# A two-layer hybrid decoder on one core: the first stage's input array in groups of eight partitions

## The chip, the cores and the metric

One of the eight cores of a Trainium2 chip runs the whole kernel. The metric is the time of one execution on the device in microseconds (us), and less is better. On the core, TensorE multiplies matrices, VectorE and ScalarE do element-wise work, GpSimd a little of it, and 16 DMA engines move data between the chip's memory (HBM) and the on-chip memory (SBUF, 128 partitions). SyncE (SP) only issues transfers; ScalarE has a queue for them too.

## The reference

Two layers of the same form, then a final normalisation, on x of 256 tokens by 1024 features, all in float32:

```python
hn = rms_norm(x, norm_gain)
proj = jnp.einsum('bsd,de->bse', hn, w_in)          # 1024 -> 3584
a_q, a_k, a_v, a_g, b_x, b_g, c_q, c_k, c_v, c_g = jnp.split(proj, _in_split_points(), axis=-1)
...
y_a = dilated_attention(qa, ka, va)... * jax.nn.silu(a_g)
y_b = rg_lru_branch(b_x, ...) * jax.nn.silu(b_g)
y_c = stick_breaking_attention(qc, kc, vc)... * jax.nn.silu(c_g)
y = jnp.concatenate([y_a, y_b, y_c], axis=-1)
return x + jnp.einsum('bse,ed->bsd', y, w_out)
```

The first stage of the kernel is two column blocks of the first layer's projection: a_v (512 columns) and c_v (256 columns), the values of the two attentions.

## The kernel before

Float32 products are made from two rounded parts each: a high part, rounded by ScalarE, and the rest, subtracted by VectorE; TensorE then adds three products (high by high, rest by high, high by rest). The kernel works through weight chunks, each loaded by SP in two halves of 512 KB into one of five staging buffers `st`, split into `whi` and `wlo`, and multiplied. TensorE's order is the order of the code; the other engines' is settled by the scheduler. A load waits until its staging buffer has been read.

The first stage runs over the 1024 features in eight tiles of 128 (`NK`, loop variable `k`), one feature a partition. A tile holds, per partition, 256 numbers of x transposed and 768 weights, 4 KB. Tile 0 comes in small pieces so that work can begin early: x with the eight columns of the norm's gain (`x0`, 264 numbers a partition, line 138), then three blocks of 256 weights (lines 139 to 141, two of them on ScalarE's queue). Tiles 1 to 7 come whole, each 512 KB, issued by SP at line 152. For each tile ScalarE rounds x times the gain into `xx` (line 161) and the weights or part of them into `whi` (lines 165 and 167), VectorE takes the rests (lines 163, 168, 170), and TensorE multiplies at line 181. Ahead of the stage TensorE runs seven multiplications of zeros (line 147).

Two arrays in HBM feed this stage: `first_x`, 128 rows of 264 numbers, and `first`, eight tiles of 128 rows of 1024 numbers, each row the 256 numbers of x and the 768 weights of one feature. Line 138 reads the first whole; lines 139 to 141 read 256 numbers of each of the 128 rows of tile 0; line 152 reads a whole tile, 128 rows that follow each other:

```python
nc.sync.dma_start(out=x0, in_=first_x)
act.dma_start(out=st0[:, S:S + 256], in_=first[0][:, S:S + 256])
...
        nc.sync.dma_start(out=st, in_=first[k])
```

After the stage SP goes on with the small parameters (line 186), the first weight chunks (line 108), the residual x (line 191), constants and rotation tables (lines 196 and 422). In each layer GpSimd issues two copies of half the partitions from one buffer on the chip to another (line 593).

Of the kernel before, what the change touches and what calls it, by code (L numbers as in the profile page):

```python
# [15 lines left out]
P = 128  # L16
S = 256
# [3 lines left out]
NK = D // P  # L21
# [11 lines left out]
STORE = (0, 256, 640, 1024)  # L33
WARM = 7

C_DG = 0
C_ID = 127
C_NM = 256
# [8 lines left out]


@with_exitstack
def trunk_kernel(ctx: ExitStack, tc: tile.TileContext, x, first_x, first, wpack, prm_d, gatew, gains, consts, rope, out):  # L50
    nc = tc.nc
    act, dve, pe, gps = nc.scalar, nc.vector, nc.tensor, nc.gpsimd

# [23 lines left out]
    def table(name, behind=()):  # L77
        load = act.preload_act_table_set(name)  # L78
        for u in (*loaded["users"], *behind):
            dep(load, u)  # L80
        loaded["load"], loaded["users"] = load, []
# [48 lines left out]
    def weights(l, c, ahead=AHEAD):  # L130
        ask(l, c, ahead)
        return ready.pop((l, c))
# [2 lines left out]
    dve.memset(cold, 0.0)  # L135
    x0 = sb.tile([P, S + NK], F32, name="x0", tag="it")
    st0 = wst.tile([P, 1024], F32, name="st", tag="st")
    nc.sync.dma_start(out=x0, in_=first_x)
    act.dma_start(out=st0[:, S:S + 256], in_=first[0][:, S:S + 256])
    nc.sync.dma_start(out=st0[:, S + 256:S + 512], in_=first[0][:, S + 256:S + 512])  # L140
    act.dma_start(out=st0[:, S + 512:1024], in_=first[0][:, S + 512:1024])
    table(LN_EXP)
    av_ps = [bank(at, "s") for _ in range(NT)]
    cv_bk = [bank(pp, "pp") for _ in range(NT)]
# [4 lines left out]
    for k in range(NK):  # L149
        st = st0 if k == 0 else wst.tile([P, 1024], F32, name="st", tag="st")  # L150
        if k > 0:
            nc.sync.dma_start(out=st, in_=first[k])
        x_in = x0 if k == 0 else st
        g = x0[:, S + k:S + k + 1]
        if k % 2 == 0:
            pair = [wsp.tile([P, 2048], F32R, name=n, tag=n) for n in ("whi", "wlo")]
        o = k % 2
        hi, cl, lo = pair[0][:, o * 1024:o * 1024 + 768], pair[0][:, o * 1024 + 768:o * 1024 + 1024], pair[1][:, o * 512:o * 512 + 512]
        both = pair[0][:, o * 1024 + 512:o * 1024 + 1024]
        w = st[:, S:1024]  # L160
        act.activation(xh[:, k, :], x_in[:, 0:S], AF.Copy, scale=g)  # L161
        for c0, c1 in {0: ((0, 256), (256, 512)), 1: ((0, 512),)}.get(k, ()):
            dve.tensor_copy(hi[:, c0:c1], w[:, c0:c1])
        if k < 2:
            act.activation(hi[:, 512:768], w[:, 512:768], AF.Copy)
        else:
            act.activation(hi, w, AF.Copy)
        dve.scalar_tensor_tensor(xl[:, k, :], x_in[:, 0:S], g, xh[:, k, :].bitcast(F32), ALU.mult, ALU.subtract)
        for rest, c0, c1 in ((lo, 0, 512), (cl, 512, 768)):
            dve.tensor_sub(rest, w[:, c0:c1], hi[:, c0:c1].bitcast(F32))  # L170
        cuts = (0, 256, 512) if k == 0 else (0, 512)
        av = [[(av_ps, c0, c1, a, b[:, c0:c1]) for c0, c1 in zip(cuts, cuts[1:])]
              for a, b in ((xh, hi), (xl, hi), (xh, lo))]
        cv = [[(cv_bk, 0, 256, a, hi[:, 512:768])] for a in (xh, xl)] + [[(cv_bk, 256, 512, xh, cl)]]
        if k < 2:
            seq = [m for i in range(3) for m in (*av[i], *cv[i])]
        else:
            seq = [m for i in range(3) for m in av[i]] + [(cv_bk, 0, 512, xh, both), *cv[1]]
        for i, (ps, c0, c1, a, b) in enumerate(seq):
            for t in range(NT):  # L180
                pe.matmul(ps[t][:, c0:c1], a[:, k, t * P:(t + 1) * P], b,  # L181
                          start=k == 0 and all(m[0] is not ps for m in seq[:i]),
                          stop=k == NK - 1 and all(m[0] is not ps for m in seq[i + 1:]), skip_group_check=True)
# [10 lines left out]
    nmask = con[:, C_NM:C_NM + 384]  # L194
    diag = con[:, C_DG:C_DG + 255]
    nc.sync.dma_start(out=con, in_=consts)
# [114 lines left out]
    for l in range(L):  # L311
# [394 lines left out]
        for n2 in range(2):  # L706
            w = weights(l, CH_O + n2)
# [41 lines left out]
def _shape_constants():  # L749
    f = np.float32  # L750
    con = np.zeros((P, C_W), f)
    con[:, C_ID:C_ID + P] = np.eye(P, dtype=f)
    nm = np.full((P, 384), -8 * BIG, f)
    for t0, c0, n in ((0, 0, 128), (128, 128, 256)):
        d = (t0 + np.arange(P))[:, None] - np.arange(n)[None, :]
        c = (d <= 128).astype(int) + (d % 4 == 0) + (d % 16 == 0)
        c = np.where(d >= 0, c, 0)
        nm[:, c0:c0 + n] = np.where(c > 0, 8 * np.log(np.maximum(c, 1).astype(np.float64)), -8 * BIG)
    con[:, C_NM:C_NM + 384] = nm
    return con  # L760
# [17 lines left out]
def _pack_weights(w_in, w_out):  # L778
    wp = np.empty((L, NCH, P, 2048), np.float32)
    narrow = ((CH_CV, 3072), (CH_BX, 2048), (CH_BG, 2304), (CH_AG, 1536), (CH_AG + 1, 1792), (CH_CG, 3328),  # L780
              (CH_CQ, 2560), (CH_CK, 2816), (CH_AQ[0], 0), (CH_AQ[1], 256), (CH_AK[0], 512), (CH_AK[1], 768))
    yk = (6, 7, 4, 5, 0, 1, 2, 3)
    for l in range(L):
        wi = w_in[l].reshape(NK, P, 3584)
        for h in range(2):
            wp[l, CH_AV + h] = wi[4 * h:4 * h + 4, :, 1024:1536].transpose(1, 0, 2).reshape(P, 2048)
        for c, col in narrow:
            blk = wi[:, :, col:col + 256]
            if c in CH_AQ + CH_AK:
                blk = blk.reshape(NK, P, 4, 2, 32).transpose(0, 1, 3, 2, 4).reshape(NK, P, 256)  # L790
            wp[l, c] = blk.transpose(1, 0, 2).reshape(P, 2048)
        wo = w_out[l].reshape(NK, P, D)
        for h in range(2):
            for n in range(2):
                blk = np.stack([wo[k, :, n * 512:n * 512 + 512] for k in yk[4 * h:4 * h + 4]])
                wp[l, CH_O + 2 * h + n] = blk.transpose(1, 0, 2).reshape(P, 2048)
    return wp


def _pack_small(conv_w, conv_b, gate_a_w, gate_a_b, gate_x_w, gate_x_b, lru_lambda):  # L800
    pr = np.zeros((P, L * SM_P), np.float32)
    gw = np.zeros((P, L, SM_W), np.float32)
    for l in range(L):
        for b in range(2):
            r = slice(b * P, b * P + P)
            o = l * SM_P + 8 * b
            pr[:, o:o + 4] = conv_w[l][:, r].T
            pr[:, o + 4] = conv_b[l][r]
            pr[:, o + 5] = gate_a_b[l].reshape(-1)[r]
            pr[:, o + 6] = gate_x_b[l].reshape(-1)[r]  # L810
            pr[:, o + 7] = lru_lambda[l][r]
            for g, w in enumerate((gate_a_w, gate_x_w)):
                c = (g * 2 + b) * P
                for j in range(2):
                    gw[(j ^ g) * HD:((j ^ g) + 1) * HD, l, c + j * HD:c + (j + 1) * HD] = w[l, 2 * b + j]
    return pr, gw


def _arrays(x, norm_gain, w_in, conv_w, conv_b, gate_a_w, gate_a_b, gate_x_w, gate_x_b,
            lru_lambda, w_out, final_gain):  # L820
    x, norm_gain, w_in, conv_w, conv_b, gate_a_w, gate_a_b, gate_x_w, gate_x_b, lru_lambda, w_out, final_gain = [
        np.asarray(a) for a in (x, norm_gain, w_in, conv_w, conv_b, gate_a_w, gate_a_b, gate_x_w, gate_x_b,
                                lru_lambda, w_out, final_gain)]
    x2 = x.reshape(S, D)
    pr, gw = _pack_small(conv_w, conv_b, gate_a_w, gate_a_b, gate_x_w, gate_x_b, lru_lambda)
    return {
        "x_in": np.ascontiguousarray(x2),
        "first_x": np.concatenate([x2.T[0:P], norm_gain[0].reshape(NK, P).T], 1),
        "first": np.concatenate([x2.T.reshape(NK, P, S), w_in[0].reshape(NK, P, 3584)[:, :, 1024:1536],
                                 w_in[0].reshape(NK, P, 3584)[:, :, 3072:3328]], 2),  # L830
        "w_pack": _pack_weights(w_in, w_out),
        "prm": pr,
        "gate_w": gw,
        "gains": np.concatenate([norm_gain[1:], final_gain[None]], 0),
        "consts": _shape_constants(),
        "rope": _rope_table(),
    }
# [16 lines left out]
```

## Time and profile before

| what | value |
|---|---|
| median of three runs | 246.11 us (246.09 to 246.35) |
| the profiled execution's own time | 246.06 us |
| its span, first to last instruction | 244.2 us |
| TensorE busy | 236.2 us (97%) |
| VectorE, ScalarE busy | 200.0 us (82%), 174.4 us (71%) |
| moved by DMA | 43.89 MB, mean 180 GB/s |
| granted TensorE clock | 0.999 |

In the rows below PE is TensorE's matmul, PEld its weight load, DVE VectorE, ACT ScalarE, POOL GpSimd, SP SyncE; a `q` behind an engine's name is its queue of transfers. L152 is line 152. A row of the timeline has start, length, engine, line, operation and tiles (written <- read), and in brackets the engine's idle time before it with what ended that.

### The profile page before, as it was taken

The page shows a single profiled execution, that of the slowest core. Times are in us where ns is not written, and L with a number is a line of the kernel's source. Part 1 is how long each engine was busy: PE and PEld are TensorE (multiplying, and loading weights), DVE is VectorE, ACT ScalarE, POOL GpSimd, SP SyncE. Part 2 cuts the span into 40 slices and gives each one's busy share as a digit, 9 for nine tenths or more (in the row PEclk, how much of TensorE's full clock was granted, in tenths as well). Part 3 has the DMA queues.
Part 4 walks back from the last instruction along what each step waited for, and adds up shares of the span by engine and source line. Part 5 has one row for each costly group of instructions (what it writes and reads, how often), then busy time and mean ns, then how long its engine had stood idle before and what let it go on. Part 6 is the DMA issues. An engine that isn't in the chain of part 4 may idle for free.

```text
span 244.2 us, 4576 instructions
## 1 busy us (share of the span) xinstructions
PE 236.2 (97%) x1651; PEld 206.6 (85%) x1651; DVE 200.0 (82%) x480; ACT 174.4 (71%) x384; POOL 10.5 (4%) x43
## 2 busy tenths in 40 slices
PE   8799999999999999999999999999999999999991
PEld 4588999999999798878888888888888878887881
DVE  3694699999999889999495585999999986997362
ACT  3677987919597689994673674876669867998143
POOL 0017200002000000000000000000010000000000
PEclk9999999999999999999999999999999999999999
DMA  6989988565846843068448288615470771000022
GB/s 193 377 254 390 384 268 291 190 205 177 240 152 207 272 153 105 1 195 320 175 134 273 88 289 268 199 44 177 171 214 7 226 282 63 31 0 0 3 75 97
DMA packets 14037, 43.89 MB, mean 180 GB/s; under 512 B 1728, under 2 KB 3008, under 8 KB 14016
## 3 DMA queue, kind: packets, MB, share of 16 engines
q1 hardware_dynamic: 13248, 42.43, 51.9%
q0 software_dynamic: 192, 0.52, 0.8%
q10 hardware_dynamic: 576, 0.66, 0.7%
q8 instruction: 13, 0.21, 0.4%
q14 instruction: 8, 0.07, 0.1%
HBM read 42.03 MB, written 1.05 MB: 176 GB/s over the span
## 4 chain that ended last, share of the span: by engine, by line
PE 94%; DMA 3%; DVE 1%; SPq 0%; ACT 0%; issue 0%; DVEq 0%
PE pp L225 34%; PE pp L344 20%; PE pp L341 10%; PE s L225 9%; PE s L181 4%; PE s L489 3%; DMA st<-first 3%; PE y L453 2%; PE pp L383 2%; PE s L542 2%; PE pp L181 2%; PE s L469 1%; PE y L225 1%; PE pp L453 1%; PE s L601 1%; PE s L273 1%
## 5 line engine op out<-in xcount | busy, mean ns | idle before, releaser
L117 DVE TENSOR_TENSOR wlo<-st,whi 128x512 fp32r<-128x512 f32 x128 | 81.8, 684 | 7.5 <-ACT whi L115 6.9
L115 ACT ACTIVATE whi<-st 128x512 fp32r<-128x512 f32 x130 | 72.5, 627 | 9.0 <-DMA st<-w_pack 3.4
L344 PE MATMUL pp<-xx,whi 128*128 128x512 f32 x208 | 50.8, 393 | 0.0
L344 PEld LDWEIGHTS pp<-xx,whi 128*128 128x128 f32 x208 | 37.8, 188 | 7.6 <-DVE q L349 0.3
L225 PE MATMUL pp<-xx,whi 128*128 128x256 f32 x288 | 38.2, 285 | 0.0
L225 PEld LDWEIGHTS pp<-xx,whi 128*128 128x128 f32 x288 | 35.8, 191 | 0.8 <-issue 0.3
L341 PEld LDWEIGHTS pp<-xx,wlo 128*128 128x128 f32 x208 | 26.9, 191 | 1.6 <-ACT scr L84 0.3
L341 PE MATMUL pp<-xx,wlo 128*128 128x256 f32 x208 | 28.0, 284 | 0.0
L225 PE MATMUL pp<-xx,wlo 128*128 128x256 f32 x144 | 20.2, 283 | 0.0
L84 ACT ACTIVATE pr<-scr,mn 128x128 f32<-128x128 f32 (+1 forms) x32 | 14.1, 443 | 6.6 <-DVE mn L549 6.6
L225 PEld LDWEIGHTS pp<-xx,wlo 128*128 128x128 f32 x144 | 18.6, 192 | 0.0
L78 ACT ACT_TABLE_LOAD x13 | 16.7, 1283 | 1.9 <-PEq L847 1.7
L347 ACT ACTIVATE low<-pp 128x256 f32<-128x256 f32 x26 | 9.4, 373 | 8.8 <-PE pp L344 8.0
L225 PE MATMUL pp<-whi,yh 128*128 128x512 f32 (+1 forms) x48 | 14.1, 382 | 0.0
L225 PE MATMUL pp<-wlo,yh 128*128 128x512 f32 (+1 forms) x48 | 13.7, 372 | 0.0
L225 PE MATMUL pp<-whi,yl 128*128 128x512 f32 (+1 forms) x48 | 13.6, 371 | 0.0
L181 PE MATMUL s<-whi,xx 128*128 128x512 f32 (+1 forms) x36 | 9.6, 384 | 1.8 <-ACT xx L161 1.7
L225 PEld LDWEIGHTS pp<-whi,yl 128*128 128x128 f32 x48 | 8.6, 188 | 1.6
L225 PEld LDWEIGHTS pp<-wlo,yh 128*128 128x128 f32 x48 | 8.6, 188 | 1.6
L225 PEld LDWEIGHTS pp<-whi,yh 128*128 128x128 f32 x48 | 8.3, 188 | 1.6 <-issue 0.3
L549 DVE CUSTOM_DVE_ANT_0 scr<-s,con 128x128 f32<-128x128 f32 (+1 forms) x32 | 9.2, 350 | 0.0
L181 PEld LDWEIGHTS s<-whi,xx 128*128 128x128 f32 x36 | 6.0, 197 | 3.3 <-ACT xx L161 2.5
(189 smaller groups left out, 372.3 us busy)
## 6 DMA issues: line engine op xcount, KB each, us to landing
st<-w_pack SPq DMA_DIRECT2D x66, 512.0 KB, 5.3
st<-first SPq DMA_DIRECT2D x7, 512.0 KB, 7.0
xres<-x_in SPq DMA_DIRECT2D x4, 256.0 KB, 7.5
gw_t<-gate_w SPq DMA_DIRECT2D x2, 256.0 KB, 6.8
gn<-gains SPq DMA_DIRECT2D x2, 256.0 KB, 5.9
xs<-xc POOLq DMA_DIRECT2D x4, 128.0 KB, 3.8
gf<-gains SPq DMA_DIRECT2D x2, 256.0 KB, 5.4
out<-st ACTq DMA_DIRECT2D x2, 192.0 KB, 2.0
```

The lines of the kernel that those rows point to most:

```text
L78: load = act.preload_act_table_set(name)
L84: i = dep(act.activation(*a, **k), loaded["load"])
L115: split[l, c] = act.activation(h, part, AF.Copy)
L117: dve.tensor_sub(r, part, h.bitcast(F32))
L181: pe.matmul(ps[t][:, c0:c1], a[:, k, t * P:(t + 1) * P], b, start=k == 0 and all(m[0] is not ps for m in seq[:i]), stop=k == NK - 1 and al ...
L225: pe.matmul(ps, a(k), b(k), start=first and i == 0, stop=last and i == len(seq) - 1, skip_group_check=skip)
L341: pe.matmul(ps[:, 0:S], lo[:, k, cs], xh[:, k, :], start=i == 0, stop=i == len(seq) - 1, skip_group_check=True)
L344: pe.matmul(ps, hi[:, k, cs], xx[:, k].rearrange("p h t -> p (h t)"), start=i == 0, stop=i == len(seq) - 1, skip_group_check=True)
L347: act.activation(low, ps[:, S:2 * S], AF.Copy, scale=sc)
L453: pe.matmul(y[hr, p * 128 + o:p * 128 + 256], vt[:, s0, hs], wts[i][s0], start=s0 == 0, stop=s0 == 1)
L489: pe.transpose(tp[:, i * P:(i + 1) * P], tiles[h0 + h][:, j * P:(j + 1) * P], ident)
L549: dve.tensor_tensor_reduce(xs[:, cs], sps[h][:, cs], nmask[:, cs], -0.125, 3e38, ALU.add, ALU.min, mn[:, t:t + 1])
```

## The change

The two arrays become one, `first`, of 16 rows of 66,624 numbers (266,496 bytes). Row e holds everything that partitions 8e to 8e + 7 get in the first stage, in the order in which it is loaded: their eight rows of x with the gain, their eight rows of the first block of 256 weights, of the second and of the third, and then for each of the seven tiles their eight rows of 1024. At its end stand 1024 zeros. Each load takes a stretch of all 16 rows and reads it as 16 x 8 rows into 128 partitions. What is loaded into which place, in which order and on which queue stays as it was.

```diff
+FIRST_W = 8 * (NK + NK * 1024) + 1024
...
-    nc.sync.dma_start(out=x0, in_=first_x)
-    act.dma_start(out=st0[:, S:S + 256], in_=first[0][:, S:S + 256])
-    nc.sync.dma_start(out=st0[:, S + 256:S + 512], in_=first[0][:, S + 256:S + 512])
-    act.dma_start(out=st0[:, S + 512:1024], in_=first[0][:, S + 512:1024])
+    def block(q, to, at_, n):
+        q.dma_start(out=to, in_=first[:, 8 * at_:8 * (at_ + n)].rearrange("e (r c) -> e r c", r=8))
+
+    block(nc.sync, x0, 0, S + NK)
+    block(act, st0[:, S:S + 256], S + NK, 256)
+    block(nc.sync, st0[:, S + 256:S + 512], S + NK + 256, 256)
+    block(act, st0[:, S + 512:1024], S + NK + 512, 256)
...
-            nc.sync.dma_start(out=st, in_=first[k])
+            block(nc.sync, st, NK + k * 1024, 1024)
...
+def _pack_first(xt, gain, wi):
+    w = np.concatenate([wi[:, :, 1024:1536], wi[:, :, 3072:3328]], 2)
+    parts = [np.concatenate([xt[0], gain.reshape(NK, P).T], 1), w[0, :, 0:256], w[0, :, 256:512], w[0, :, 512:768]]
+    parts += [np.concatenate([xt[k], w[k]], 1) for k in range(1, NK)]
+    rows = [a.reshape(P // 8, -1) for a in parts]
+    flat = np.concatenate(rows, 1)
+    out = np.zeros((P // 8, FIRST_W), np.float32)
+    out[:, 0:flat.shape[1]] = flat
+    return out
```

The arrays are laid out ahead of the launch. In the order of instructions, SP's queue at the start of the program stands so before (a row is a line, the transfer's target and source, and the target's shape as the instruction carries it):

```order
L138 DMA x_84<-first_x 128x264
L140 DMA st<-first 128x256
L152 DMA st<-first 128x1024 x7
L186 DMA prm_t<-prm 128x32
L108 DMA st<-w_pack 128x1024 x2
```

and so with the change:

```order
L140 DMA x_84<-first 128x1x264
L140 DMA st<-first 128x1x256
L140 DMA st<-first 128x1x1024 x7
L190 DMA prm_t<-prm 128x32
L109 DMA st<-w_pack 128x1024 x2
```

No transfer has moved; the shapes of the first stage's transfers have a level more, and the lines behind have shifted by a few. ScalarE's two transfers change in the same way, and the other engines' orders are the same.

More of the change, by code (lines that the diff above doesn't have):

```diff
@@ L49, in trunk_kernel @@
 @with_exitstack
-def trunk_kernel(ctx: ExitStack, tc: tile.TileContext, x, first_x, first, wpack, prm_d, gatew, gains, consts, rope, out):
+def trunk_kernel(ctx: ExitStack, tc: tile.TileContext, x, first, wpack, prm_d, gatew, gains, consts, rope, out):
     nc = tc.nc
@@ L827, in _arrays @@
         "x_in": np.ascontiguousarray(x2),
-        "first_x": np.concatenate([x2.T[0:P], norm_gain[0].reshape(NK, P).T], 1),
-        "first": np.concatenate([x2.T.reshape(NK, P, S), w_in[0].reshape(NK, P, 3584)[:, :, 1024:1536],
-                                 w_in[0].reshape(NK, P, 3584)[:, :, 3072:3328]], 2),
+        "first": _pack_first(x2.T.reshape(NK, P, S), norm_gain[0], w_in[0].reshape(NK, P, 3584)),
         "w_pack": _pack_weights(w_in, w_out),
```

## The prediction

> **What bounds the kernel now.** I read the busy times first, then the stages, then the one wait that the stages point to, then the transfers behind that wait. Of the stage rows the first number is the length, the second TensorE's busy time; the last two are the busy share of the DMA engines and the rate in GB/s.
>
> ```profile
> span 244.2 us, 4576 instructions
> PE 236.2 (97%) x1651; PEld 206.6 (85%) x1651; DVE 200.0 (82%) x480; ACT 174.4 (71%) x384; POOL 10.5 (4%) x43
> ...
> 4.10:6.80 2.70, 2.69 (x19) 2.46 (x18) 1.63 (x4) 0.42 (x1) 0.00 (x0) 1.00 0.85 302
> 6.80:8.50 1.70, 0.02 (x1) 0.04 (x1) 0.56 (x2) 0.59 (x2) 0.00 (x0) 1.00 1.01 410
> 8.50:23.40 14.90, 14.82 (x72) 12.33 (x73) 12.35 (x29) 11.58 (x23) 4.79 (x14) 1.00 0.94 326
> 23.40:60.00 36.60, 36.60 (x336) 35.70 (x335) 32.84 (x71) 28.07 (x57) 2.80 (x16) 1.00 0.73 258
> 60.00:120.00 60.00, 60.00 (x448) 53.02 (x445) 53.84 (x140) 46.69 (x108) 1.21 (x3) 1.00 0.58 189
> 120.00:236.00 116.00, 116.00 (x754) 99.23 (x753) 94.22 (x223) 82.21 (x185) 1.31 (x3) 1.00 0.40 130
> ```
>
> TensorE is the bound at full clock: from 8.5 to 236 us it never stands still. The one hole inside the work is 6.8 to 8.5. Whatever moves the end of that hole moves the end of the kernel by as much, in both directions; an earlier end is worth 1.69 us at most. The timeline says what ends it:
>
> ```profile
> 3.51 0.51 ACT L161 ACTIVATE xx<-x 128x256 fp32r<-128x256 f32 x1 [0.56 <-DMA x<-first_x]
> 4.13 0.92 PE L181 MATMUL s<-whi,xx 128*128 128x256 f32 x4
> ...
> 7.91 0.51 ACT L161 ACTIVATE xx<-st,x 128x256 fp32r<-128x256 f32 x1 [3.10 <-DMA st<-first]
> 8.48 0.72 PE L181 MATMUL s<-whi,xx 128*128 128x512 f32 x2 [1.69 <-ACT xx L161]
> 9.57 0.83 ACT L167 ACTIVATE whi<-st 128x768 fp32r<-128x768 f32 x1
> 11.03 1.09 PE L181 MATMUL s<-whi,xx 128*128 128x512 f32 x4
> 13.10 1.09 PE L181 MATMUL s<-whi,xx 128*128 128x512 f32 x4
> ...
> 1.64 6.25 DMA st<-first
> ```
>
> Tile 1 (the first 512 KB tile; tile 0 is the small pieces) is issued at 1.64 and lands 6.25 us later (last row, from the chain of waits), at 7.89. ScalarE rounds its x at 7.91, and TensorE, done with tile 0, starts at 8.48. From tile 2 on TensorE takes 2.07 us a tile (11.03 to 13.10), and tile 2's rounding ends at 9.57 + 0.83 = 10.40, that is 0.63 us before TensorE wants it: later tiles have slack, tile 1 has none.
>
> **What the change touches.** The eleven issues of the first stage read another address pattern; no instruction of an engine that computes is added, removed or moved. So there are two costs to find: the issue itself, and how fast the bytes come.
>
> ```profile
> L152 SPq DMA_DIRECT2D st<-first x7: 327/424/468, 1.6 to 11.5; - x7
> L138 SPq DMA_DIRECT2D x<-first_x x1: 367/367/367, 0.7 to 0.7; - x1
> L139 ACTq DMA_DIRECT2D st<-first x1: 413/413/413, 0.7 to 0.7; - x1
> L191 SPq DMA_DIRECT2D xres<-x_in x4: 425/602/708, 14.6 to 16.4; - x4
> L422 SPq DMA_DIRECT2D rp<-rope x1: 1218/1218/1218, 21.8 to 21.8; - x1
> ...
> x<-first_x SPq DMA_DIRECT2D x1, 132.0 KB, 2.7
> st<-first SPq DMA_DIRECT2D x1, 128.0 KB, 2.9
> st<-first ACTq DMA_DIRECT2D x2, 128.0 KB, 3.1
> st<-first SPq DMA_DIRECT2D x7, 512.0 KB, 7.0
> ```
>
> **The issue.** Every issue of before has a source and a target of 128 rows; now the source is 16 groups of 8 rows and the target 128 rows of one piece, so the two sides no longer match and the queue has more to work out. No row of before has such a form. The lower end is no change (367 to 468 ns, and no reason for less). The upper end is the longest issue of this queue, 1.22 us, 0.85 more than the 0.37 of x's. I take +0.2 us an issue, the median 602 ns of L191 against the 424 of L152, because those are issues of the same queue under load. Every transfer of the stage then starts at least 0.2 us later, since x's is the first. Tile 1's own issue would end 0.6 later, but it has cover:
>
> ```profile
> 1.18 0.45 ACTq L141 DMA_DIRECT2D st<-first  x1
> ...
> DMA to landing us min/median/max: 3.5/5.3/8.9
> ```
>
> The second row is of the weight loads (line 108), also 512 KB: the quickest landed 3.5 us after its issue began. Tile 1, issued at 1.64, could so have been there at 5.1 and lands at 7.89; what is ahead of it, the small pieces (the last, of 1.18, landed 3.1 later, at 4.3), and the stall below hold it, not its issue. Term: **+0.2 us** on tile 1, with 0 as one end. The other end is issues of 1.22 us with no cover: tile 1's issue ends at 0.74 + 3 x 1.22 = 4.4 and not at 1.64 + 0.42, +2.3. The same 0.2 on tile 0 is hidden by the hole of 1.69.
>
> **The rate.** Before tile 1 is there, 132 + 3 x 128 + 512 = 1028 KB = 1.053 MB have to move. Two stretches show what the DMA engines deliver when they are always busy:
>
> ```profile
> 8.50:10.50 2.00, 1.92 (x9) 1.53 (x10) 1.76 (x5) 1.56 (x4) 0.00 (x0) 1.00 1.02 418
> 180.30:181.30 1.00, 1.00 (x8) 0.88 (x7) 1.00 (x10) 1.00 (x5) 0.00 (x0) 1.00 1.00 242
> ...
> q1 hardware_dynamic: 92, 0.36, 67.3%
> q0 software_dynamic: 57, 0.14, 30.9%
> ```
>
> The first is tiles of this stage, 128 rows onto 128 partitions: 418 GB/s. The second has the copies of line 593 in flight (the software queue q0; the last two rows are the queues' shares in 180.3 to 182.3), 64 rows onto 64 partitions, beside a weight load: the engines are as busy and deliver 242, 0.58 of it. So a transfer's rate here hangs on which partitions the 16 DMA engines write at one time. The new form fixes that: the source has 16 groups, one for each engine if they are dealt out in order, so that an engine writes eight consecutive partitions. Today's dealing is not in the trace, but its 418 says that it is one without collisions. For the new one there are two bounds: no collision, 1.053 MB / 418 = 2.52 us as now, or collisions all the time, 1.053 / 242 = 4.35 us, which is 1.83 more. [...]
>
> [...]
>
> **Later tiles.** [...] At full collision a tile takes 2.17, tile 2 is 0.3 late and each of the next five 0.1: +0.8. Behind the stage nothing is added, since the loads wait for buffers that the work itself frees, and move with it:
>
> ```profile
> SPq L108 <- DVE wlo L117: 119.1, 50, 12.7
> ```
>
> **Sum.** Tile 1 lands 0.2 + 1.4 us later, and the end moves by 1.6. The profiled execution took 246.06 (span 244.2 and 1.86 around it); the median of the runs shown, 246.11, is 0.05 above, which I leave out. 246.06 + 1.6 = **247.7 us**. Its own range is 246.7 (a third of the collisions) to 248.9 (all of them, 1.83 + 0.2 + 0.8).
>
> **The rivals.** Anything within 0.2% (0.5 us) of the time before is about what a measurement of this kernel cannot tell from no change.
>
> *Smoother reads: faster.* Tile 1 is late today by more than its bytes explain. Behind the last small piece (4.3 us) a 512 KB tile needs 1.25 us at 418 GB/s and would be there at 5.6; it lands at 7.89, 2.3 later. The rate from 1.6 to 9.0 us, in 40 slices of 0.185 us, shows where:
>
> ```profile
> DMA  3927789999999348987998789988999999999999
> GB/s 23 108 40 256 282 285 300 339 316 388 366 299 188 133 177 266 288 332 266 354 244 354 288 354 376 354 332 332 376 399 465 376 376 421 443 421 443 376 399 443
> ```
>
> Between 3.8 and 4.4 it drops to 133 to 188, just as the engines go from the small pieces to the rows of tile 1. If that stall comes from where the rows lie in HBM, another pitch (266,496 bytes from group to group instead of rows that follow each other) may end it. Half of the 2.3 us back, less 0.2 for the issues, gives 246.06 - 0.95 = 245.1; the hole caps it at 244.6. It decides against me if tile 1 lands before 7.9. Against it speaks that the old layout runs at 418 five microseconds later, so nothing in it is slow as such.
>
> [...]
>
> *Nothing but the issues: the same.* If the engines are dealt their partitions as today, only +0.2 is left: 246.3. For it: both sides still move the same bytes in 128 rows. Against it: the source can no longer be walked as one run of 128 rows.
>
> *The stage becomes DMA bound: much slower.* Issues of 1.22 us without cover (+2.3) and full collisions (1.83 + 0.8 = +2.6) together give 251.0. Only if both upper ends hold.
>
> **Chances.** Collisions 0.55, only the issues 0.22, smoother reads 0.18, both upper ends 0.05. The range 245.1 to 248.8 leaves out the better half of the smoother reads, the worst case, and a little of the likeliest: under 2 in 10. Faster by over 0.2%: 0.18; within: 0.22; slower: 0.60.
>
> **What would show it.** Right: issues of 0.5 to 0.7 us in the first stage; a rate well under 418 GB/s with busy DMA engines from 4 to 12 us; TensorE's hole before tile 1 from 1.7 to 3 us or more. Wrong: issues as long as before; 418 GB/s in the same stretch; tile 1 landing before 7.9 us and a hole under 1.7. A stall between 3.8 and 4.4 us that is gone would speak for the smoother reads.

## The result and the profile after

The changed kernel took 248.75 us (median of 6 runs, 247.9 to 249.86) against 246.23 for the kernel before: a ratio of 1.0119, 95% interval 1.0089 to 1.0148. Ratios are of the fast runs alone: this one leaves out an execution of the kernel before of 1327.31 us, which its median counts, and one further down leaves out one of 249.42. Slower, as forecast, but by more (247.7 was forecast, with a range to 248.8; 246.06 times the ratio is 249.0), and not in the way forecast. The profiled execution took 249.38 us, with a span of 247.1 us against 244.2.

The stages of the changed kernel, in the columns of the prediction's stage rows:

```profile
4.10:6.80 2.70, 1.73 (x5) 1.00 (x4) 1.31 (x4) 0.04 (x1) 0.00 (x0) 1.00 0.88 238
6.80:8.50 1.70, 0.12 (x1) 0.13 (x1) 0.14 (x1) 0.59 (x2) 0.00 (x0) 1.00 1.04 274
8.50:10.50 2.00, 2.00 (x10) 2.00 (x11) 1.97 (x5) 0.82 (x3) 0.00 (x0) 1.00 1.03 258
8.50:12.00 3.50, 3.50 (x16) 3.40 (x17) 3.04 (x7) 1.77 (x4) 0.00 (x0) 1.00 1.03 255
12.00:23.40 11.40, 11.40 (x56) 9.62 (x55) 8.68 (x21) 7.75 (x14) 1.15 (x3) 1.00 1.03 296
```

The rate is what the prediction feared: DMA engines as busy as before deliver 274 GB/s from 6.8 to 8.5 us and 258 from 8.5 to 10.5, where they gave 410 and 418. (From 8.5 to 12 us, the stretch of the rows below, the kernel before has 368, since its engines are less busy at the end of it; 418 is its first 2 us.) But TensorE's idle stretch has grown to the left: it already lacks 0.97 us in 4.1 to 6.8, where before it lacked 0.01. TensorE's waits and its timeline tell for what:

```profile
PE pp L185 <- ACT whi L169: 2.1, 1, 2.1
PE s L185 <- DVE whi L167: 0.4, 1, 0.4
```

```profile
5.43 0.80 PE L185 MATMUL s<-whi,xx 128*128 128x256 f32 x2 [0.40 <-DVE whi L167]
8.38 0.80 PE L185 MATMUL pp<-whi,xx 128*128 128x256 f32 x2 [2.14 <-ACT whi L169]
8.97 1.05 PE L185 MATMUL s<-whi,xx 128*128 128x256 f32 x4
9.82 0.63 PE L185 MATMUL pp<-whi,xx 128*128 128x256 f32 x2
10.25 1.05 PE L185 MATMUL s<-wlo,xx 128*128 128x256 f32 x4
11.10 0.63 PE L185 MATMUL pp<-whi,xx 128*128 128x256 f32 x2
11.53 1.05 PE L185 MATMUL s<-whi,xx 128*128 128x512 f32 x2
...
26.63 2.08 PE L229 MATMUL pp<-xx,whi 128*128 128x256 f32 x16
```

The same work in the kernel before (its wait ahead of tile 1, at 8.48, stands in the prediction):

```profile
4.89 0.47 PE L181 MATMUL pp<-whi,xx 128*128 128x256 f32 x2
5.20 0.64 PE L181 MATMUL s<-whi,xx 128*128 128x256 f32 x4
5.68 0.40 PE L181 MATMUL pp<-whi,xx 128*128 128x256 f32 x2
5.91 0.64 PE L181 MATMUL s<-wlo,xx 128*128 128x256 f32 x4
6.39 0.40 PE L181 MATMUL pp<-whi,xx 128*128 128x256 f32 x2
...
23.47 2.08 PE L225 MATMUL pp<-xx,whi 128*128 128x256 f32 x16
```

`pp<-whi` at the top of both lists is the first work on tile 0's third small block (line 169 rounds it). It starts at 8.38 instead of 4.89. There is no hole ahead of tile 1 any more: tile 1 (11.53) waits behind tile 0. Three things are read here, and the experiments take them one by one.

- *The wait.* 8.38 - 4.89 = 3.49 us later, of which the old hole of 1.69 takes up a part: 1.80 us are left.
- *The speed.* The rest of tile 0 takes 11.53 - 8.38 = 3.15 us instead of about 1.90 (4.89 to the end of the last pair at 6.79): a pair of 128x256 takes 0.63 to 0.80 us instead of 0.40. (TensorE was slow ahead of the long wait already: the pair at 5.43 takes 0.80 too.) That is 1.25 us more, and 1.80 + 1.25 = 3.05 is by how much TensorE's tile 1 is late (11.53 against 8.48).
- *What follows.* The stage (to the first multiplication of line 229, before 225) ends 3.16 us later; from there to the end of the span it is 247.1 - 26.63 = 220.47 us, before 220.73. So the span grows by 2.9.

ScalarE's rows and the issues:

```profile
7.91 0.42 ACT L169 ACTIVATE whi<-st 128x256 fp32r<-128x256 f32 x1 [3.77 <-DMA st<-first]
8.23 0.49 ACT L165 ACTIVATE xx<-st,x 128x256 fp32r<-128x256 f32 x1
...
10.21 0.51 ACT L165 ACTIVATE xx<-st,x 128x256 fp32r<-128x256 f32 x1 [1.18 <-DMA st<-first]
12.24 0.51 ACT L165 ACTIVATE xx<-st,x 128x256 fp32r<-128x256 f32 x1 [0.79 <-DMA st<-first]
```

```profile
L140 SPq DMA_DIRECT2D st<-first x8: 536/584/802, 1.5 to 12.6; - x8
L140 ACTq DMA_DIRECT2D st<-first x2: 657/762/867, 0.8 to 1.4; - x2
L140 SPq DMA_DIRECT2D x<-first x1: 655/655/655, 0.7 to 0.7; - x1
```

Tile 1's x is rounded at 8.23 with no wait of its own (before, 7.91), so tile 1 was there by then: at most 0.34 us later than the 7.89 of before, not 1.6. The third small block was there only at 7.9; before, ScalarE had it at 4.39. It was issued at 1.44 by ScalarE's queue in 0.87 us (0.45 before), and tile 1's issue on SP began at 2.08. What the block then met shows in the packets of the queues between 4.1 and 7.1 us (packets, MB, share of the engines' time; q1 is SP's queue, q10 ScalarE's). With the change:

```profile
q1 hardware_dynamic: 183, 0.66, 81.3%
q10 hardware_dynamic: 71, 0.06, 8.7%
```

and before, where ScalarE's queue has nothing left in this stretch:

```profile
q1 hardware_dynamic: 253, 0.93, 86.7%
```

About half of the block's 0.13 MB moves only now, while SP's queue moves the rows of tile 1.

### The profile page after: what moved, and what is told of

The parts are those of the page before. It is cut to its first block, busy times and chain, and to the rows that moved or that the text cites. A ratio compares the mean times of both kernels' runs of the same rounds, so it can differ in the third digit from the quotient of the medians.

```text
span 247.1 us, 4576 instructions
## 1 busy us (share of the span) xinstructions
PE 238.3 (96%) x1651; PEld 208.5 (84%) x1651; DVE 200.6 (81%) x480; ACT 174.2 (70%) x384; POOL 10.9 (4%) x43
## 4 chain that ended last, share of the span: by engine, by line
PE 95%; DMA 3%; ACT 0%; ACTq 0%; issue 0%; DVE 0%; DVEq 0%
PE pp L229 34%; PE pp L348 19%; PE pp L345 10%; PE s L229 9%; PE s L185 5%; PE s L493 3%; PE pp L185 3%; DMA st<-first 3%; PE y L457 2%; PE pp L387 2%; PE s L546 2%; PE s L473 1%; PE y L229 1%; PE pp L457 1%; PE s L605 1%; PE s L277 1%
## 5 line engine op out<-in xcount | busy, mean ns | idle before, releaser
L229 PE MATMUL pp<-whi,yl 128*128 128x512 f32 (+1 forms) x48 | 13.6, 371 | 0.0
L185 PE MATMUL s<-whi,xx 128*128 128x512 f32 (+1 forms) x36 | 10.9, 421 | 0.4 <-DVE whi L167 0.4
L185 PEld LDWEIGHTS pp<-whi,xx 128*128 128x128 f32 x36 | 7.5, 218 | 3.8 <-ACT whi L169 2.4
L185 PE MATMUL pp<-whi,xx 128*128 128x256 f32 (+1 forms) x36 | 8.5, 349 | 2.1 <-ACT whi L169 2.1
```

The costliest lines, as they stand in the source:

```text
L185: pe.matmul(ps[t][:, c0:c1], a[:, k, t * P:(t + 1) * P], b, start=k == 0 and all(m[0] is not ps for m in seq[:i]), stop=k == NK - 1 and al ...
L229: pe.matmul(ps, a(k), b(k), start=first and i == 0, stop=last and i == len(seq) - 1, skip_group_check=skip)
```

## The experiments

Every ratio is to the kernel before on the same chip. Single executions of one kernel differ by 3 to 4 us in several kernels here, so a profile is read for what happened in it, and medians for the time.

### What sets the rate: pitch, form or dealing

**Groups near each other.** The new 16 x 8 form, but each group's piece only 256 bytes behind the one before it, and each load one stretch of memory.

```diff
-        q.dma_start(out=to, in_=first[:, 8 * at_:8 * (at_ + n)].rearrange("e (r c) -> e r c", r=8))
+        g = 8 * n + 64
+        src = first[0, at_:at_ + 16 * g].rearrange("(e w) -> e w", e=16)[:, 0:8 * n]
+        q.dma_start(out=to, in_=src.rearrange("e (r c) -> e r c", r=8))
```

> The new form (16 groups of 8 rows) on rows that lie nearly as before: piece by piece, one group 256 bytes behind the other. If the form deals each DMA engine eight consecutive partitions and engines meet, the stage stays slow: 250 to 265 GB/s from 8.5 to 12 us with busy engines, and 248 to 250 us. If the wide pitch in HBM (266,496 bytes) made the reads slow, the rate is back at 400 to 430 GB/s and the time is 246 to 247 us, the longer issues (0.6 us) alone being left.

Measured: 248.0 us, ratio 1.0149 (1.0115 to 1.0184). Its row of 8.5 to 12 us:

```profile
8.50:12.00 3.50, 3.50 (x16) 3.40 (x17) 3.46 (x9) 2.50 (x6) 0.00 (x0) 0.50 1.01 331
```

As slow as the change, though memory is read almost in one run: the pitch of 266,496 bytes isn't the cause of the time. The rate, 331 GB/s, lies between the two that were expected, and the granted clock (the third number from the end) is 0.50.

**Rows laid out by partition, old form.** Each partition's pieces follow one another, 128 rows of 32,800 bytes, and each load takes a stretch of each row.

```diff
-        q.dma_start(out=to, in_=first[:, 8 * at_:8 * (at_ + n)].rearrange("e (r c) -> e r c", r=8))
+        q.dma_start(out=to, in_=first[:, at_:at_ + n])
```

> All that a partition gets in the first stage lies together (128 rows of 32,800 bytes), read in the old form, 128 rows onto 128 partitions. If the form is the cause: 400 to 430 GB/s from 8.5 to 10.5 us, issues of 0.33 to 0.47 us, third small block landed by 4.5 us, 245.3 to 246.7 us. If rows that lie far apart in HBM are the cause: under 300 GB/s and 248 us or more. If smoother reads were to be had from another layout: tile 1 lands before 7 us and the time is under 245.6.

Measured: 245.54 us, ratio 1.0033 (0.9997 to 1.0069).

```profile
8.50:12.00 3.50, 3.42 (x18) 2.81 (x17) 3.27 (x9) 3.50 (x6) 0.00 (x0) 1.00 1.02 417
```

Rows scattered over HBM come at 417 GB/s, and the issues take 0.33 to 0.55 us. So in the old form neither time nor rate hung on where the rows lie here (before, 368 GB/s in this stretch, and 418 in its first 2 us); a neutral version, not a better one.

**The old form in 120 and 8 rows.** The arrays of before, each tile in two loads. That 120 rows are shared out among the engines otherwise than 128 was the author's guess.

```diff
-            nc.sync.dma_start(out=st, in_=first[k])
+            for p in (slice(0, 120), slice(120, P)):
+                nc.sync.dma_start(out=st[p], in_=first[k][p])
```

> The kernel before, old arrays and old form, but each tile in two loads, of 120 rows and of 8. [...] If the dealing is the cause: 200 to 320 GB/s with busy engines between 6 and 12 us though form and layout are the old ones. If the three-level form or the layout is: 350 or more.

Measured (one execution): 249.46 us.

```profile
8.50:12.00 3.50, 3.16 (x14) 2.45 (x15) 2.60 (x6) 1.74 (x4) 0.00 (x0) 1.00 0.96 246
```

**The old form in two halves.** The arrays of before, two loads of 64 partitions per tile.

```diff
-            nc.sync.dma_start(out=st, in_=first[k])
+            for h in range(2):
+                nc.sync.dma_start(out=st[h * 64:h * 64 + 64], in_=first[k][h * 64:h * 64 + 64])
```

> The kernel before with each tile in two loads of 64 partitions, old arrays and old form. If the DMA engines slow each other by the partitions that they write: 200 to 260 GB/s with busy engines between 6 and 12 us, as in the copies of 64 partitions. If not: 350 or more.

Measured (one execution): 248.49 us.

```profile
8.50:12.00 3.50, 3.20 (x16) 2.45 (x15) 2.41 (x6) 1.32 (x3) 0.00 (x0) 1.00 1.04 239
```

Old array, old two-level form, and the same low rate at busy engines, once the set of partitions that a load covers is changed. Together with the kernel of rows (417) this speaks against array and place as the cause of the low rate, and for the way in which the partitions are shared out among the DMA engines. It rests on one execution each, and each tile also comes in two loads here; engines busy 0.96 to 1.04 of the time speak against a cost of the number of loads. No view shows which engine wrote which partition: that the sharing out is the cause, and that engines meet, is the author's inference.

The 239 GB/s of the halves are 0.57 of the 417 of the rows, as the copies of 64 partitions had 0.58 of 418.

**Two loads more, meant to put engines out of step.** Two odd-sized loads on ScalarE's queue, meant to delay some engines against others (they fill part of `xres`, which is loaded later anyway).

```diff
+    xres = cst.tile([P, NT, D], F32, name="xres")
+    for p0, n, w in ((0, 24, 2048), (32, 68, 256)):
+        act.dma_start(out=xres[p0:p0 + n].rearrange("p t d -> p (t d)")[:, 0:w], in_=wpack[1, 0][p0:p0 + n, 0:w])
```

> [...] If the reads or the form itself are slow whoever else writes: 250 to 265 as before. The time says nothing, since ScalarE issues more.

Measured (one execution): 253.42 us, 259 GB/s from 8.5 to 12, within the 250 to 265 expected if the reads or the form are slow. But the rows of the added loads ran from 5.5 to 13.6 us, in among those of the tiles, so nothing shows that the engines were out of step as meant: inconclusive.

### Which part of the change costs: small pieces, tiles, or both

**Only the small pieces in the new form** (tiles 1 to 7 read as before).

```diff
-            block(nc.sync, st, NK + k * 1024, 1024)
+            nc.sync.dma_start(out=st, in_=first1[k])
```

> Only the four small pieces in the new form; the seven tiles are read as before from an array of their own. If the slow rate of the tiles is what makes the changed kernel late (its tiles and all loads behind them): 410 GB/s or more from 8.5 to 10.5 us, tile 7 landed by 17 us, and at most 0.4% over before. If the late third small block alone is enough: it lands after 6 us, TensorE waits for it, and the time stays 0.8% or more over before.

Measured: 247.45 us, ratio 1.0078 (1.005 to 1.0107). Its tiles come at 373 GB/s from 8.5 to 12 (before, 368), and yet its profiled execution, one of its slowest (249.74), has the wait of the changed kernel:

```profile
PE pp L185 <- ACT whi L169: 1.5, 1, 1.5
```

**Only the tiles in the new form** (the small pieces read as before).

```diff
-    block(nc.sync, x0, 0, S + NK)
-    block(act, st0[:, S:S + 256], S + NK, 256)
+    nc.sync.dma_start(out=x0, in_=first_x)
+    act.dma_start(out=st0[:, S:S + 256], in_=first0[:, S:S + 256])
...
```

> Only the seven tiles in the new form; the small pieces as before. If the tiles' rate is enough: 240 to 340 GB/s from 8.5 to 12 us, TensorE's first stage ends 1 to 2 us late, a second wait shows between 28 and 34 us since the weight loads queue behind the tiles, and the time is 0.8 to 1.6% over before. If the third block was what counted: under 0.4% over before.

Measured: 247.33 us, ratio 1.0048 (1.0017 to 1.008), single executions from 245.23 to 249.42. Once more on another chip:

> The small pieces in the old form, the tiles in the new one, once more. Theory A (engines meet at the partitions in some executions and not in others): the rate between 8.5 and 20 us differs by over 30 GB/s from the 330 of the last profile, or the times of single executions spread over more than 2 us. Rival B (each layout has its own fixed rate): 320 to 340 GB/s again, and times within 1 us of each other.

Measured: 247.69 us (246.7 to 248.37), ratio 1.009 (1.0058 to 1.0121). The rate from 8.5 to 12 us was 330 GB/s in the first profile (an execution of 245.23 us) and 257 in the second (246.94). By the measure set beforehand theory A holds. But the two profiles come from two chips, and on the second one all five with the tiles in the new form lie between 245 and 269 GB/s: whether the execution or the chip decides the rate stays open. In neither profile did the stage end 1 to 2 us late, as the first expectation had it (22.72 and 23.15 us, before 23.47), and the third small block was rounded on time, at 4.15 and 4.25.

Over all repeats, each half of the change costs 0.5 to 1.1% by itself, and both together 1.2 to 1.5%: either half is enough, so there are two causes.

### The third small block

**Third block on SP.** The changed kernel, with the third block ahead of tile 1 on SP's queue instead of on ScalarE's.

```diff
-    block(act, st0[:, S + 512:1024], S + NK + 512, 256)
+    block(nc.sync, st0[:, S + 512:1024], S + NK + 512, 256)
```

> The changed kernel with the third small block on SP's queue, ahead of tile 1, in place of ScalarE's. If the end is set by that block, whose rows take turns with tile 1's slow rows on the same engines: it lands by 5.5 us, TensorE's tile 1 starts near 9.3 us instead of 11.5, and the time falls to 246.8 to 247.6 us, at the same 257 GB/s. If the end is set by tile 1's own landing and the rate of the tiles, as forecast: no change, 248 to 249.9 us.

Measured: 248.5 us, ratio 1.0168 (1.0139 to 1.0197). The block was there at 5.03, TensorE's tile 1 starts 2.57 us earlier than in the changed kernel and the stage ends at 24.23 instead of 26.63:

```profile
8.96 0.71 PE L185 MATMUL s<-whi,xx 128*128 128x512 f32 x2 [1.41 <-ACT xx L165]
```

The time didn't follow. TensorE now waits in the next stage, on weights:

```profile
PEld pp L229 <- ACT whi L116: 1.2, 4, 0.5
```

Both once more, on one chip, the changed kernel first:

> The changed kernel once more, as the measure for the others on this chip: 247.9 to 249.9 us, 1.2% (0.9 to 1.5) over the kernel before; 250 to 340 GB/s between 8.5 and 12 us, the third small block of tile 0 landing after 7 us.

> The changed kernel with tile 0's third small block on SP's queue, as before. Theory A (the late stream of loads alone costs as much as the late third block): within 0.4% of the changed kernel, with TensorE's tile 1 starting at about 9 us instead of 11.5. Theory B (the late third block alone costs the 1.2%): at least 1 us below the changed kernel, within 0.7% of the kernel before.

Measured: the changed kernel 249.21 us, ratio 1.0147 (1.012 to 1.0173); with the third block on SP 248.59, ratio 1.0128 (1.0096 to 1.016): 0.25% apart, as theory A says. The block was there at 6.11 this time. TensorE's tile 1 starts at 8.83 instead of 11.07 and the stage ends 1.4 us earlier (24.77 against 26.20), but the rest takes 222.5 us instead of 220.5. From the chain of waits of the kernel with the block on SP:

```profile
7.01 9.92 DMA st<-first
...
18.47 8.59 DMA xres<-x_in
...
30.81 1.04 ACT whi L116 x2
...
33.24 2.42 PE pp L229 x18
```

The tiles come late, SP issues the residual x and the weights behind them, ScalarE gets to its statistics and to rounding the weights later, and TensorE waits at 33 us, far behind the stage. The late block and the late loads are two limits that lie about equally far back, so taking away either leaves the other.

**Small pieces alone, third block on SP.**

> The tiles in the old form, the small pieces in the new one, and the third piece on SP's queue ahead of tile 1. Theory A (what is lost with the small pieces alone is the third piece that takes turns with tile 1's rows): it lands by 5.5 us and the time is 0 to 0.4% over the kernel before. Rival B (the longer issues, 0.2 to 0.4 us each, cost by themselves): 0.7% or more over, although the piece lands by 5.5 us.

Measured: 247.22 us, ratio 1.0074 (1.0047 to 1.0101). The block was there at 6.03, not by 5.5, and the median is rival B's: a block ahead of tile 1 on the same queue still comes third there, behind longer issues (it is issued at 2.09). Its TensorE waits only 1.17 us, but slows down soon after (a pair of 128x256 at 0.63 us from 8.49, granted clock 0.50 there).

### Why TensorE is slow behind the wait

**The hole filled.** Five further multiplications of the zero tile where TensorE stands idle in tile 0: one ahead of the second group, four ahead of the third block's. Nothing reads them.

```diff
         for i, (ps, c0, c1, a, b) in enumerate(seq):
+            for _ in range({1: 1, 2: 4}.get(i, 0) if k == 0 else 0):
+                pe.matmul(warm, cold[:, 0:P], cold, start=True, stop=True)
```

> The changed kernel once more, as the measure for the filled one on this chip: 0.9 to 1.5% over the kernel before, tile 0's rest at 2.9 to 3.2 us, and 220.5 us from the stage's end to the end of the span.

> The changed kernel with five further matmuls of 128x512 bf16 on the zero tile in TensorE's hole of tile 0 (one ahead of the second group of tile 0, four ahead of the third block's), so that TensorE does not stand idle there. Theory A (the idle hole costs clock): two matmuls of 128x256 take 0.40 to 0.50 us after the wait instead of 0.63 to 0.80, tile 0's rest takes 1.9 to 2.2 us instead of 3.15, the stage ends 0.8 to 1.3 us earlier than in the changed kernel; the time falls by as much at most, and by less where the late loads then set the end (220.5 us from the stage's end grows to 221 to 222.5). Rival B (the matmuls are long for another reason of the late block): they stay at 0.63 or more and the time is the same within 0.3%, or longer by up to 1 us for the added work.

Measured: the changed kernel 249.56 us, ratio 1.0148 (1.0091 to 1.0205); filled 249.03, ratio 1.015 (1.0127 to 1.0174). In the filled kernel's timeline:

```profile
8.75 0.51 PE L187 MATMUL pp<-whi,xx 128*128 128x256 f32 x2 [1.14 <-ACT whi L169]
9.09 0.64 PE L187 MATMUL s<-whi,xx 128*128 128x256 f32 x4
9.57 0.40 PE L187 MATMUL pp<-whi,xx 128*128 128x256 f32 x2
...
10.53 0.63 PE L187 MATMUL s<-whi,xx 128*128 128x512 f32 x2
...
25.04 2.08 PE L231 MATMUL pp<-xx,whi 128*128 128x256 f32 x16
```

and in that of the changed kernel beside it:

```profile
8.88 0.80 PE L185 MATMUL pp<-whi,xx 128*128 128x256 f32 x2 [1.66 <-ACT whi L169]
...
12.04 1.05 PE L185 MATMUL s<-whi,xx 128*128 128x512 f32 x2
...
27.04 2.08 PE L229 MATMUL pp<-xx,whi 128*128 128x256 f32 x16
```

The third block came as late as ever, yet tile 0's rest takes 10.53 - 8.75 = 1.78 us, where the changed kernel beside it takes 12.04 - 8.88 = 3.16, and the stage ends 2.0 us earlier (25.04 against 27.04; 0.13 of it is the earlier start). So, by one profile each, TensorE is quick behind the wait with work in the hole of tile 0, and slow without. The long wait alone need not be what slows it, and the slow work need not come at once: in the first profile of the changed kernel the pair ahead of the long wait was slow already, and in its first repeat (26.20 above) TensorE was quick right behind a wait of 2.86 us and slow from about 9 us on:

```profile
8.37 0.51 PE L185 MATMUL pp<-whi,xx 128*128 128x256 f32 x2 [2.86 <-ACT whi L169]
...
9.37 0.63 PE L185 MATMUL pp<-whi,xx 128*128 128x256 f32 x2
```

The time stays, since the late loads catch it (222.2 us from there to the end, in the changed kernel 220.5):

```profile
PE pp L231 <- ACT whi L116: 0.6, 2, 0.3
```

The changed kernel's stage row gives a granted clock of 1.00 from 8.5 to 12 us all the same, and two others in this study 0.50 and 0.56 for the same slow multiplications (the groups near each other and the changed kernel's first repeat); the mean time of a multiplication was the surer reading. By it TensorE runs at little more than half its speed: four multiplications of 128x256 take 0.85 us (8.97 to 9.82 in the changed kernel) against 0.48 (5.20 to 5.68 before). The length of a wait doesn't tell whether slow work follows. One of 1.69 us (before) was followed by a first pair of 128x512 at 0.72 us and then by pairs of 128x256 at 0.39 to 0.40, one of 1.17 (the small pieces with the block on SP) by pairs at 0.63 from 8.49 us on, and that of 2.86 in the repeat above by a first pair at 0.51 and then pairs at 0.63 from 9.37 us on. No idle stretch in these kernels' tile 0 was longer than 2.86 us. Beyond that the runs don't show what makes TensorE slow, or when it sets in.

**The small pieces alone, filled,** with the unfilled kernel on the same chip.

> The kernel of small pieces alone once more, as the measure for the filled one on this chip: 0.5 to 1.1% over the kernel before, the third block landing after 7 us, and pairs of 128x256 at 0.63 us or more behind the wait.

> The tiles in the old form, the small pieces in the new one, and the same five matmuls in the hole. Theory A: the pairs of 128x256 behind the wait take 0.40 to 0.50 us instead of 0.63 to 0.79, and since the loads are on time here, the time falls by 0.8 to 1.3 us against the same kernel without them, to 0.2 to 0.4% over the kernel before. Rival B: within 0.2% of the kernel without them, or above.

Measured: unfilled 248.32 us (245.68 to 249.18), filled 248.2 (246.74 to 248.59). No difference, which is rival B's forecast, so these runs don't show that the slow work costs the kernel time. The reason can't be seen, since both profiled executions were of the kind in which the third block came in time. That itself tells something. The unfilled one's profile (245.68 us, the quickest of its four):

```profile
L140 ACTq DMA_DIRECT2D st<-first x2: 613/630/647, 0.8 to 1.4; - x2
```

```profile
2.36 0.60 SPq L156 DMA_DIRECT2D st<-first  x1
5.83 0.42 ACT L169 ACTIVATE whi<-st 128x256 fp32r<-128x256 f32 x1 [1.48 <-DMA st<-first]
```

and the profile of the same kernel's first run (249.74 us):

```profile
L140 ACTq DMA_DIRECT2D st<-first x2: 670/766/862, 0.8 to 1.5; - x2
```

```profile
2.09 0.58 SPq L156 DMA_DIRECT2D st<-first  x1
7.75 0.42 ACT L169 ACTIVATE whi<-st 128x256 fp32r<-128x256 f32 x1 [3.60 <-DMA st<-first]
```

With 0.61 us for its issue (the second of the queue) the third block was there at 5.83, with 0.86 at 7.75. The rows of line 156 are tile 1's issue: in the quick execution it begins at 2.36, after the block's issue has ended (2.04), in the late one at 2.09, before that end (2.32). In the quick one the second block's issue on SP's queue is the long one instead, 0.83 us against 0.57, and TensorE waits 1.3 us for that block. In six profiles in which the third block came after 7.7 us on ScalarE's queue (the changed kernel three times, the filled one, the small pieces alone and the groups near each other) its issue took 0.86 to 0.87; the kernel with the two added loads is an exception, with 0.70 and the block at 8.30. A quarter of a microsecond in the issue goes with 1.9 us in the landing. That a late block's rows of 1 KB take turns with tile 1's rows of 4 KB fits this, the packets by queue shown above, and the block's 5.03 and 6.11 on SP's queue; no view lists rows by engine, so the turns themselves are inferred.

## Why the prediction was wrong

The direction was right, the size and the mechanism were not. The profiled executions, with the stage's end (first multiplication behind it) and what is left of the span:

| kernel | time, us | stage ends | rest |
|---|---|---|---|
| before | 246.06 | 23.47 | 220.73 |
| changed | 249.38 | 26.63 | 220.47 |
| changed, hole filled | 249.55 | 25.04 | 222.16 |
| changed, third block on SP (second) | 249.28 | 24.77 | 222.53 |
| only tiles in the new form (second) | 246.94 | 23.15 | 221.85 |
| rows by partition | 245.59 | 22.66 | 220.44 |

- *The issue, +0.2 us each.* Right: 0.54 to 0.87 us against 0.33 to 0.47, that is 0.2 to 0.4 more.
- *"The same 0.2 on tile 0 is hidden by the hole of 1.69."* **This step failed.** Tile 0's delay was 3.49 us, not 0.2: its third block sits on a second queue, whose issue grew by 0.4, so that it moved beside tile 1's rows (0.06 MB of it between 4.1 and 7.1 us). (With the small pieces in the old form it was rounded at 4.15 and 4.25 us, though the tiles were in the new one.) The prediction followed the longer issues along SP's queue and not on to what the other queue's block would meet. Of the delay 1.80 us went past the hole, and 1.25 were added by TensorE at little more than half speed (0.85 us for four multiplications instead of 0.48), which the prediction didn't have: there an idle TensorE cost only the time it stood idle.
- *Collisions, 418 to between 418 and 242 GB/s.* Right as to the rate (238 to 274 in the changed kernel from 4.1 to 12 us; the lower bound of 242, read from copies within the chip, came back as 239 in the loads of halves). That the dealing of the partitions is the cause, and that engines collide over them, is the author's inference: the kernels of 120 rows (246) and of halves (239) fit it, and no view shows it. No run shows the term of +1.4 us: in its place stand a rate near the lower bound and a tile 1 hardly later. Wrong as to what it does: *"Tile 1 lands 0.2 + 1.4 us later"*; it was there at most 0.34 later. With the third block on SP's queue, ahead of it, its x was rounded at 8.38 and 8.26, still only 0.4 to 0.5 later than before. Tile 1's landing of before held 2.3 us that its bytes don't explain, as the rival of smoother reads had noted; in the changed kernel these must have shrunk by about what the lower rate added. Why, no run here shows.
- *Later tiles.* 2.17 us a tile was worked out for full collision; 2.03 were measured (10.21 to 12.24), still less than TensorE's 2.07.
- *"Behind the stage nothing is added, since the loads wait for buffers that the work itself frees."* **Failed too.** The residual x and the weights queue behind the tiles on SP. In the changed kernel this is covered by the late third block; where that is taken away it shows as 1.4 to 2.1 us more rest.
- *The rivals.* Smoother reads (faster) and only issues (the same) are ruled out by time and rate. Both upper ends (251.0) had a rate near the measured one but not the issues (0.87 at most, not 1.22).
- *What would show it.* A hole of 1.7 to 3 us ahead of tile 1 was named; the hole was 2.14 + 0.40 us, but inside tile 0, which tells another story.

So the sum was mis-sized at its cover: +1.6 on tile 1 with tile 0 free, where the chip gave +3.05 through tile 0 with tile 1 all but free.

## What to carry to other kernels

When transfers of one buffer lie on two queues, follow each queue's longer issues to the last piece that the work needs, and ask whose rows it will meet (here an issue of 0.87 us instead of 0.45, and a block rounded at 7.91 instead of 4.39); a hole that is to hide a delay must be checked against that piece. Look for slow work around an idle stretch of TensorE (here it moved a stage's end by 2 us, and the median by no more than the scatter), and read that from the mean time of a multiplication, not from the granted clock alone. If taking away a wait moves a stage's end but not the kernel's, subtract the stage's end from the span: a rest that grows (here 222.5 us against 220.5) says that a second limit lay just behind.

## What was not expected of the hardware

- The same load form ran at 330 GB/s in one execution and at 257 in another, on another chip, with engines busy 1.03 of the time in both.
- Five multiplications of zeros in the idle stretch brought the work behind it from 3.16 to 1.78 us, but left the kernel's time about where it was (249.03 us against 249.56).
- In one and the same kernel the second issue of ScalarE's queue took 0.61 us in one execution and 0.86 in another, on two chips, and the block landed 1.9 us apart.
